# Half of an instance norm's stores moved from ScalarE's queue to GpSimd's

## The chip, the core and the metric

The kernel runs on one core of a Trainium2 chip. The metric is the device time of one execution in microseconds; the lower the better.

## The reference

`x` has the shape (4, 8, 16, 256, 256) in float32, that is 512 channels of 65,536 values, 134 MB in all. Every channel is brought to mean 0 and variance 1, and multiplied by its gamma.

```python
mu = x.mean(axis=(3, 4), keepdims=True)
var = ((x - mu) ** 2).mean(axis=(3, 4), keepdims=True)
x_norm = (x - mu) / np.sqrt(var + 1e-5)
out = x_norm * gamma[None, :, :, None, None]
```

## The kernel before

The 512 channels are cut into 32 units (`U`) of 16 channels. A unit is a tile of 128 partitions x 8192 floats (4 MB, one contiguous row of 32 KB for each partition): eight partitions hold one channel. Six tiles in SBUF, `slots` (`xt` in the profile), are used in turn: unit `u` lives in slot `u % 6`, and `AHEAD` is 6.

A unit goes through these steps:

1. Load (L48, in the helper `load`). The first six loads are issued at the start: units 0, 2, 4 and 5 by SP (SyncE), 1 and 3 by ACT (ScalarE). Every later load is issued by SP.
2. DVE (VectorE) sums each row (L107) while ACT squares it and sums the squares (L108; the squares themselves go to `junk`).
3. A small matmul with `navg` (L116) adds up the eight partitions of a channel, which gives minus the mean and minus the mean square.
4. DVE, ACT and DVE make the variance (L117), its root (L121), the reciprocal (L125) and the scale (L127), all 128 x 1.
5. DVE adds minus the mean and multiplies by the scale, in place (L130).
6. The store (L134) is issued by ACT, on ACT's queue.
7. SP issues the load of unit `u + 6` into the same slot (L136), which has to wait until the store of `u` has landed.

The order is the program's, engine by engine: nothing is moved by a scheduler, and semaphores are set where data depends on data. SP, ACT and GpSimd each have a DMA queue of their own; SP's and ACT's are listed in the profile as hardware queues (q1 and q10), GpSimd's as a software queue (q0). All three are served by the same 16 DMA engines. GpSimd's queue carries two small transfers at the start: `touch`, 16 rows of 512 B written into the output's first tile (L54) ahead of that tile's store, and `g_row`, the load of gamma (L55). After its six loads are issued, the program has 60 no-ops on ACT.

Of the kernel before, what the change touches and what calls it, by code (L numbers as in the profile page):

```python
# [1 line left out]

# [4 lines left out]

F32 = mybir.dt.float32
U8 = mybir.dt.uint8
ALU = mybir.AluOpType  # L10
ACTF = mybir.ActivationFunctionType
AX = mybir.AxisListType


@with_exitstack
def kernel(
    ctx: ExitStack,
    tc: tile.TileContext,
    x: bass.AP,
    gamma: bass.AP,  # L20
    out: bass.AP,
):
    nc = tc.nc
    B, G, C, H, W = x.shape
    P = nc.NUM_PARTITIONS
    HW = H * W
    n_ch = B * G * C
    S = 8
    K = P // S
    F = HW // S  # L30
    U = n_ch // K
    NG = (G * C) // K
    AHEAD = 6
    assert HW % S == 0 and (G * C) % K == 0

    xv = x.rearrange("b g c h w -> (b g c h w)").rearrange("(u p f) -> u p f", p=P, f=F)
    ov = out.rearrange("b g c h w -> (b g c h w)").rearrange("(u p f) -> u p f", p=P, f=F)
    gv = gamma.rearrange("g c -> (g c)")

    data = ctx.enter_context(tc.tile_pool(name="data", bufs=1))  # L40
    singles = ctx.enter_context(tc.tile_pool(name="singles", bufs=1))
    psum = ctx.enter_context(tc.tile_pool(name="psum", bufs=4, space=bass.MemoryType.PSUM))
    ctx.enter_context(tc.manual_schedule())

    slots = [data.tile([P, F], F32, name=f"xt{i}") for i in range(AHEAD)]

    def load(u, queue):
        queue.dma_start(out=slots[u % AHEAD][:], in_=xv[u])  # L48


    g_row = singles.tile([1, G * C], F32, name="g_row")
    touch = singles.tile([16, 128], F32, name="touch")
    nc.vector.memset(touch[:], 0.0)  # L53
    nc.gpsimd.dma_start(out=ov[0][0::S, 0:128], in_=touch[:])  # L54
    nc.gpsimd.dma_start(out=g_row[:], in_=gv[None, :])  # L55
    for u in range(AHEAD):
        load(u, nc.scalar if u in (1, 3) else nc.sync)

    for _ in range(60):
        nc.scalar.nop()  # L60

    eps_t = singles.tile([P, 1], F32, name="eps_t")
    nc.gpsimd.memset(eps_t[:], 1e-5)
    one = singles.tile([1, 1], F32, name="one")
    nc.gpsimd.memset(one[:], 1.0)
    navg = singles.tile([P, K, S], F32, name="navg")
    nc.gpsimd.memset(navg[:], -1.0 / HW)  # L67
    nc.gpsimd.affine_select(  # L68
        out=navg[:], in_=navg[:], pattern=[[-S, K], [0, S]], compare_op=ALU.is_ge,
        fill=0.0, base=0, channel_multiplier=1,  # L70
    )
    nc.gpsimd.affine_select(  # L72
        out=navg[:], in_=navg[:], pattern=[[S, K], [0, S]], compare_op=ALU.is_ge,
        fill=0.0, base=S - 1, channel_multiplier=-1,
    )
    navg_w = navg[:].rearrange("p k s -> p (k s)")
    root_eps = singles.tile([P, 1], F32, name="root_eps")
    nc.scalar.activation(out=root_eps[:], in_=eps_t[:], func=ACTF.Sqrt)  # L78
    g_rep = singles.tile([1, NG, K, S], F32, name="g_rep")
    g_ps = psum.tile([P, NG], F32, name="g_ps", bufs=1)  # L80
    g_col = singles.tile([P, NG], F32, name="g_col")

    nc.vector.tensor_copy(  # L83
        out=g_rep[:],
        in_=g_row[:].rearrange("o (n k) -> o n k", n=NG).unsqueeze(3).to_broadcast([1, NG, K, S]),
    )
    for n in range(NG):
        nc.tensor.matmul(  # L88
            out=g_ps[:, n : n + 1],
            lhsT=g_rep[:, n].rearrange("o k s -> o (k s)"),  # L90
            rhs=one[:],
            start=True, stop=True,
        )
    nc.vector.tensor_copy(out=g_col[:], in_=g_ps[:])  # L94

    junk = singles.tile([P, F], U8, name="junk")

    st = singles.tile([P, U, 2], F32, name="st")
    nvar = singles.tile([P, U], F32, name="nvar")
    std = singles.tile([P, U], F32, name="std")  # L100
    rstd = singles.tile([P, U], F32, name="rstd")
    scale = singles.tile([P, U], F32, name="scale")

    squares = []
    for u in range(U):
        t = slots[u % AHEAD]
        nc.vector.reduce_sum(out=st[:, u, 0:1], in_=t[:], axis=AX.X)  # L107
        square = nc.scalar.activation(  # L108
            out=junk[:], in_=t[:], func=ACTF.Square, accum_out=st[:, u, 1:2],
        )  # L110
        if u:

            tc.declare_no_dep(square.ins, squares[-1].ins, reason="junk, ordered by the root between")
        squares.append(square)
        ps = psum.tile([P, 2], F32, name="ps")
        nc.tensor.matmul(out=ps[:], lhsT=navg_w, rhs=st[:, u], start=True, stop=True)  # L116
        nc.vector.tensor_scalar(  # L117
            out=nvar[:, u : u + 1], in0=ps[:, 0:1], scalar1=ps[:, 0:1],
            scalar2=ps[:, 1:2], op0=ALU.mult, op1=ALU.add,
        )  # L120
        nc.scalar.activation(  # L121
            out=std[:, u : u + 1], in_=nvar[:, u : u + 1], func=ACTF.Sqrt,
            bias=eps_t[:], scale=-1.0,
        )
        nc.vector.reciprocal(out=rstd[:, u : u + 1], in_=std[:, u : u + 1])  # L125
        g = u % NG
        nc.vector.tensor_mul(  # L127
            out=scale[:, u : u + 1], in0=rstd[:, u : u + 1], in1=g_col[:, g : g + 1],
        )
        nc.vector.tensor_scalar(  # L130
            out=t[:], in0=t[:], scalar1=ps[:, 0:1], scalar2=scale[:, u : u + 1],
            op0=ALU.add, op1=ALU.mult,
        )
        nc.scalar.dma_start(out=ov[u], in_=t[:])  # L134
        if u + AHEAD < U:
            load(u + AHEAD, nc.sync)  # L136


# [1 line left out]
_INS = ['x', 'gamma']  # L140
_OUTS = [((4, 8, 16, 256, 256), 'float32')]


# [23 lines left out]
```

## Time and profile before

| | us |
|---|---|
| runs of the kernel: lowest, median, highest | 626.88, 627.39, 627.53 |
| profiled execution: span from the first to the last instruction | 624.9 |
| profiled execution: its own time around the span | not recorded; the runs' median is 2.5 above the span |
| busy in the span: DVE | 443.4 (71%) |
| busy in the span: ACT | 238.8 (38%) |
| busy in the span: PE (matmul) | 21.4 (3%) |
| busy in the span: POOL (GpSimd) | 2.4 (0%) |
| bytes moved by DMA | 268.46 MB, mean 430 GB/s |

How to read it: the busy times are means over the whole span. The slices show where in the span an engine or the DMA was busy, each slice being a fortieth of it (15.6 us). The DMA issues are listed by what they write and read, and by the engine that issues them (SPq, ACTq, POOLq), with the median time from issue to landing; that time holds the wait in the queue as well as the transfer.

### The profile page before, as it was taken

What the parts mean: (1) busy time and instruction counts of PE and PEld (TensorE: products, weight loads), DVE (VectorE), ACT (ScalarE), POOL (GpSimd) and SP (SyncE); (2) the same over time, 40 slices, a digit from 0 to 9 for tenths busy, and PEclk for the clock granted to TensorE, in tenths of its full rate; (3) what the DMA queues carried; (4) which work ended last, traced back from release to release, by engine and by line L of the source; (5) the groups of instructions that cost most, each with busy time, mean ns of one, the idle gap of its engine ahead of it and who ended that gap; (6) DMA issues with size and microseconds to landing.
All of it is one profiled execution on the core that took longest, in us unless ns stands there. A gap on an engine that the chain in (4) does not pass through costs nothing.

```text
span 624.9 us, 631 instructions
## 1 busy us (share of the span) xinstructions
PE 21.4 (3%) x80; PEld 19.5 (3%) x80; DVE 443.4 (71%) x163; ACT 238.8 (38%) x98; POOL 2.4 (0%) x11
## 2 busy tenths in 40 slices
PE   0200000000000000000000000000000000000000
PEld 0200000000000000000000000000000000000000
DVE  0588999999776687666786767867668676687730
ACT  0444444444443234432344423444224442244400
POOL 1000000000000000000000000000000000000000
DMA  8999999999999999999999999999999999999998
GB/s 370 436 426 430 422 434 436 436 436 437 432 424 433 436 436 424 436 436 434 436 436 432 422 436 436 434 426 436 436 434 436 436 434 419 436 436 434 426 436 369
DMA packets 9282, 268.46 MB, mean 430 GB/s; under 512 B 1072, under 2 KB 1088, under 8 KB 1088
## 3 DMA queue, kind: packets, MB, share of 16 engines
q10 hardware_dynamic: 4896, 142.61, 52.9%
q1 hardware_dynamic: 4320, 125.83, 46.8%
q0 software_dynamic: 64, 0.01, 0.0%
q14 instruction: 2, 0.02, 0.0%
HBM read 134.22 MB, written 134.23 MB: 430 GB/s over the span
## 4 chain that ended last, share of the span: by engine, by line
another core or an unknown queue 61%; DMA 17%; DVE 15%; SPq 1%; PE 1%; issue 0%; ACT 0%
DVE st L107 10%; DMA xt<-in_x_dram 10%; DMA out_dram<-xt 8%; DVE xt L130 5%; SPq L48 1%; PE ps L116 1%; ACT std L121 0%; DVE nvar L117 0%; DVE rstd L125 0%; DVE scale L127 0%
## 5 line engine op out<-in xcount | busy, mean ns | idle before, releaser
L107 DVE TENSOR_REDUCE st<-xt 128x1 f32<-128x8192 f32 x32 | 277.9, 8685 | 100.4 <-DMA xt<-in_x_dram 100.4
L108 ACT ACTIVATE junk<-xt 128x8192 uint8<-128x8192 f32 x32 | 225.0, 7030 | 275.1 <-DMA xt<-in_x_dram 231.9
L130 DVE TENSOR_SCALAR xt<-xt,ps,scale 128x8192 f32<-128x8192 f32 x32 | 145.6, 4550 | 1.2
L121 ACT ACTIVATE std<-nvar,eps_t 128x1 f32<-128x1 f32 x32 | 9.4, 294 | 79.6 <-DVE nvar L117 79.6
L116 PE MATMUL ps<-st,navg 128*128 128x2 f32 x64 | 17.9, 349 | 557.1 <-DVE st L107 557.1
L116 PEld LDWEIGHTS ps<-st,navg 128*128 128x128 f32 x64 | 16.0, 311 | 558.9 <-issue 558.9
L117 DVE TENSOR_SCALAR nvar<-ps 128x1 f32<-128x1 f32 x32 | 9.2, 287 | 23.8 <-PE ps L116 23.8
L125 DVE RECIPROCAL rstd<-std 128x1 f32<-128x1 f32 x32 | 5.2, 164 | 11.6 <-ACT std L121 11.6
L83 DVE COPY g_rep<-g_row 1x1024 f32<-1x1024 f32 x1 | 0.7, 681 | 14.3 <-DMA g_row<-in_gamma_dram 14.3
L108 ACT ACTIVATION_READ_ACCUMULATOR junk<-xt 128x1 f32 x32 | 6.0, 186 | 0.0
L127 DVE TENSOR_TENSOR scale<-rstd,g_col 128x1 f32<-128x1 f32 x32 | 5.1, 159 | 1.1
L88 PE MATMUL g_ps<-one,g_rep 1*128 1x1 f32 x16 | 3.5, 347 | 16.1 <-DVE g_rep L83 16.1
L88 PEld LDWEIGHTS g_ps<-one,g_rep 1*128 1x128 f32 x16 | 3.5, 325 | 16.1 <-issue 16.1
L94 DVE COPY g_col<-g_ps 128x8 f32<-128x8 f32 x1 | 0.2, 166 | 3.7 <-PE g_ps L88 3.7
L78 ACT ACT_TABLE_LOAD x1 | 1.3, 1283 | 1.7 <-PEq L151 1.7
L53 DVE MEMSET touch<- 16x128 f32 x1 | 0.2, 165 | 0.9 <-PEq L151 0.9
L54 POOL DMA_DIRECT2D out_dram<-touch x1 | 0.6, 619 | 0.8 <-DVE touch L53 0.8
L55 POOL DMA_DIRECT2D g_row<-in_gamma_dram x1 | 0.5, 487 | 0.0
L68 POOL TENSOR_SCALAR_AFFINE_SELECT navg<-navg 128x128 f32<-128x128 f32 x1 | 0.4, 400 | 0.1
L72 POOL TENSOR_SCALAR_AFFINE_SELECT navg<-navg 128x128 f32<-128x128 f32 x1 | 0.4, 399 | 0.1
L67 POOL MEMSET navg<- 128x128 f32 x1 | 0.2, 232 | 0.0
L78 ACT ACTIVATE root_eps<-eps_t 128x1 f32<-128x1 f32 x1 | 0.2, 203 | 0.0
(6 smaller groups left out, 0.6 us busy)
## 6 DMA issues: line engine op xcount, KB each, us to landing
out_dram<-xt ACTq DMA_DIRECT2D x32, 4096.0 KB, 62.5
xt<-in_x_dram SPq DMA_DIRECT2D x30, 4096.0 KB, 38.5
xt<-in_x_dram ACTq DMA_DIRECT2D x2, 4096.0 KB, 31.5
out_dram<-touch POOLq DMA_DIRECT2D x1, 8.0 KB, 9.1
g_row<-in_gamma_dram POOLq DMA_DIRECT2D x1, 0.5 KB, 13.3
```

The lines of the kernel that those rows point to most:

```text
L48: queue.dma_start(out=slots[u % AHEAD][:], in_=xv[u])
L78: nc.scalar.activation(out=root_eps[:], in_=eps_t[:], func=ACTF.Sqrt)
L83: nc.vector.tensor_copy(out=g_rep[:], in_=g_row[:].rearrange("o (n k) -> o n k", n=NG).unsqueeze(3).to_broadcast([1, NG, K, S]),)
L88: nc.tensor.matmul(out=g_ps[:, n : n + 1], lhsT=g_rep[:, n].rearrange("o k s -> o (k s)"), rhs=one[:], start=True, stop=True,)
L107: nc.vector.reduce_sum(out=st[:, u, 0:1], in_=t[:], axis=AX.X)
L108: square = nc.scalar.activation(out=junk[:], in_=t[:], func=ACTF.Square, accum_out=st[:, u, 1:2],)
L116: nc.tensor.matmul(out=ps[:], lhsT=navg_w, rhs=st[:, u], start=True, stop=True)
L117: nc.vector.tensor_scalar(out=nvar[:, u : u + 1], in0=ps[:, 0:1], scalar1=ps[:, 0:1], scalar2=ps[:, 1:2], op0=ALU.mult, op1=ALU.add,)
L121: nc.scalar.activation(out=std[:, u : u + 1], in_=nvar[:, u : u + 1], func=ACTF.Sqrt, bias=eps_t[:], scale=-1.0,)
L125: nc.vector.reciprocal(out=rstd[:, u : u + 1], in_=std[:, u : u + 1])
L127: nc.vector.tensor_mul(out=scale[:, u : u + 1], in0=rstd[:, u : u + 1], in1=g_col[:, g : g + 1],)
L130: nc.vector.tensor_scalar(out=t[:], in0=t[:], scalar1=ps[:, 0:1], scalar2=scale[:, u : u + 1], op0=ALU.add, op1=ALU.mult,)
```

## The change

The store of an odd unit is now issued by GpSimd, on its own queue. The store of an even unit is issued by ACT as before. The 60 no-ops on ACT are gone. Loads, tiles, arithmetic and all the rest stay, and so do the waits that data asks for: a store waits for its L130, the load of unit `u + 6` for the store of unit `u`.

```diff
     for u in range(AHEAD):
         load(u, nc.scalar if u in (1, 3) else nc.sync)
-
-    for _ in range(60):
-        nc.scalar.nop()
...
             op0=ALU.add, op1=ALU.mult,
         )
-        nc.scalar.dma_start(out=ov[u], in_=t[:])
+        (nc.gpsimd if u % 2 else nc.scalar).dma_start(out=ov[u], in_=t[:])
         if u + AHEAD < U:
             load(u + AHEAD, nc.sync)
```

GpSimd's list of instructions grows by 16 stores, behind what it did before (units 1, 3, ... 31, in this order); ACT's gets shorter by the same 16.

## The prediction

> **What bounds the kernel now.** I read the page's slices first, because DVE at 71% and ACT at 38% name no bound.
>
> ```profile
> DMA  8999999999999999999999999999999999999998
> GB/s 370 436 426 430 422 434 436 436 436 437 432 424 433 436 436 424 436 436 434 436 436 432 422 436 436 434 426 436 436 434 436 436 434 419 436 436 434 426 436 369
> ...
> q10 hardware_dynamic: 4896, 142.61, 52.9%
> q1 hardware_dynamic: 4320, 125.83, 46.8%
> q0 software_dynamic: 64, 0.01, 0.0%
> ```
>
> The 16 DMA engines are full in all but the first and last slice. q1 is SP's queue (30 loads), q10 is ACT's (32 stores, 2 loads), and q0, GpSimd's, has almost nothing. In the trace's packet records a packet is one row of 32 KB and takes 1.213 us; the first starts at 1.80 us and the last ends at 623.6. 8192 of them on 16 engines are 512 x 1.213 = 621.1 us, against a window of 621.8. So there is nothing to win in the middle: a change can only open gaps, or close 0.7 us. Next, the queues:
>
> ```profile
> out_dram<-xt ACTq DMA_DIRECT2D x32, 4096.0 KB, 62.5
> xt<-in_x_dram SPq DMA_DIRECT2D x30, 4096.0 KB, 38.5
> ```
> ```profile
> SPq L48 <- DMA out_dram<-xt: 534.4, 26, 59.5
> ```
>
> A unit comes every 19.36 us (period of SP's issues in the chain of waits), so a 4 MB transfer alone takes 19.36 / 2 = 9.68 us. A slot spends 38.5 us on its load, 15.1 in compute and 62.5 on its store: 116.1 us, which is 6 x 19.36. The second line says that SP waits only for stores, as each load needs its slot emptied. Hence 62.5 / 19.36 = 3.2 stores and two loads are outstanding at any time. Then the end, from the timeline:
>
> ```profile
> 585.26 8.69 DVE L107 TENSOR_REDUCE st<-xt 128x1 f32<-128x8192 f32 x1 [4.35 <-DMA xt<-in_x_dram]
> ...
> 595.73 4.55 DVE L130 TENSOR_SCALAR xt<-xt,ps,scale 128x8192 f32<-128x8192 f32 x1
> 600.32 0.34 ACTq L134 DMA_DIRECT2D out_dram<-xt  x1
> ```
> ```profile
> DMA to landing us min/median/max: 23.6/62.5/62.6
> ```
>
> The last load lands at 585.24. Unit 31 is computed in 15.08 us and its store issued at 600.32; it has the shortest landing, 23.6 us, so it lands at 623.9. From 585.24 to there are 38.7 us = 4.0 stores of 9.68. That is the pile of stores 28 to 31. It keeps the engines full while unit 31 is computed: the long store queue is the cover of the tail.
>
> **The change, part by part.**
>
> *No-ops.* ACT issues its second load by 1.68 us, starts its table load at 1.72, and then waits 19.4 us for the first tile (`ACT junk` row of the waits). Whatever 60 no-ops cost there, that wait hides it: 0.
>
> *Sequencers.* An issue on ACT took 0.34 us; 16 leave it. ACT also no longer waits at odd units for L130 before it squares the next tile. Its square (7.03 us) starts with DVE's reduction (8.69 us) and ends earlier, so nothing follows from that: 0. GpSimd has 2.4 us of work, all before 4 us, so its stores queue behind nothing but their own wait for L130. SP's list stays as it is: load u+6 waits for store u, in order.
>
> *Who gets turns.* This is the part that counts. The trace of before has one place with all three queues at work, the start:
>
> ```profile
> 1.35 0.62 POOL L54 DMA_DIRECT2D out_dram<-touch  x1 [0.85 <-DVE touch L53]
> ```
>
> Its 16 small rows (and those of g_row behind them) go out in the packet records one per engine every 2.43 us, between one 32 KB packet of q1 and one of q10. So the engines give each queue with work one packet in turn, and the software queue is a third partner. Before, loads and stores had one queue each and shared 1:1 however long the store pile was, so the pile built at the start (units 0 to 5 were finished 14.93 us apart) stayed to the end. With stores in two queues, two outstanding stores get two turns of three: they drain at two per 3 x 9.68 = 29.0 us, while a new store comes only with each load, one per 29.0 us. The pile loses one store each 29 us until one is in flight; 2.2 surplus stores are gone in some 64 us, long before the end. From then on the share is 1:1, a unit still takes 19.36 us, and the six slots hold the difference as waiting loads: stores land after about 20.7 us (even) to 24.3 (odd), loads after 116.2 - 15.1 - 22.5 = 78.6. The middle costs nothing, but the cover of the tail is gone.
>
> *How late a software store starts.* A hardware load issued at 0.80 had its first packet at 1.80: 1.0 us. The software store issued at 1.35 had its first packet at 7.12; its turn at 4.70 passed unused, so it was ready 3.4 to 5.8 us after issue. That was 16 rows; with 128, the 0.62 us of its instruction may grow eightfold, by 4.3 us, or not at all. The ends are 1.0 (as hardware) and 5.8 + 4.3 = 10.1 us; I take 4.6, the middle of the only row of its kind.
>
> The Trainium skill ("DMA: Bandwidth & Descriptors", section "Latency and other measured facts") gives a first byte after about 1 us for GpSimd's path and 0.6 for the others. By that difference of 0.4 us the sum below would be about +8.7 us instead of +11.2; the touch row, at 3.4 or more, disagrees.
>
> *The tail.* At the last load's landing, these stores are still to be moved:
> - store 31: 9.68 us, not issued;
> - store 30 (even, ACT): issued 19.36 - 15.08 = 4.28 us before, started 1.0 later, half of 3.28 us moved: 8.1 left;
> - store 29 (odd, GpSimd): issued 23.6 us before, started 4.6 later; half of 15.7 and a third of 3.28 moved, 9.0 in all: 0.7 left.
>
> That is 18.5 us of work instead of 38.7. The engines were full up to there in both cases, so the last load lands 38.7 - 18.5 = 20.2 us later, at 605.4. After it come 15.08 us of compute, 4.6 to start, 9.68 of data and 0.35 to land: 29.7 us instead of 38.7. Net: +20.2 - 9.0 = **+11.2 us**. Seen as a gap: the engines run dry 8.8 us after the last load and get store 31 after 19.7, so they idle 10.9 us. With a start of 1.0 us the same lines give +21.0 - 12.6 = +8.4; with 10.1, +17.5 - 3.5 = +14.0.
>
> *Sum.* On the profiled span: 624.9 + 11.2 = 636.1. The median of the runs, 627.39, is 2.5 us above the span; that part stays, so 638.6 us.
>
> **Rivals.**
>
> *Nothing changes (the side that is not slower).* The store pile could outlive the split, if the software queue gets fewer turns than a third of them (by the row above it got exactly its turn, but with packets too small to matter). The place is the tail. The point is 15.08 + 4.6 = 19.7 us, or 2.0 stores, still queued besides store 31 when the last load lands; my sum leaves 8.8 us, before had 29.0. From there on the bytes set the end: 627.4. In its favour: the 62.5 us of landing show how deep that pile is today.
>
> The Trainium skill (same page, "Issuing engines are not separate DMA queues") says that issuing from several engines only saves the sequencer's issue time; read by itself it forecasts this case. The trace agrees on the shared engines, and shows beside it that the number of queues sets the share.
>
> *Software packets smaller than a row.* If 32 KB rows are cut into k packets, the odd stores get 1/k of a turn, their pile stays, and the tail is mostly covered; but each packet costs about 8 ns more (the 512-byte packets took 27 ns, their bytes at 27 GB/s take 19). 128 odd rows per engine x (k-1) x 8 ns: 3.1 us at k=4, 7.2 at k=8; at k=2 1 us and a good half of the gap, some 6. So 630.5 to 635. Against it: touch went out as whole rows of 512 B; for it: no row of before shows a large software packet.
>
> *Software stores start far later.* If making 128 rows' descriptors takes eight times the touch store's time and more, each odd store holds its slot longer, and store 31 pays it in full: +14.0 and above, 641.4 to 646. For it: 5.8 us were possible with 16 rows. Against: the instruction itself took only 0.62 us.
>
> *Faster.* By over 0.2% (1.25 us, about what a measurement can tell here) would need more than the 0.7 us of slack in the DMA window, so packets under 1.21 us.
>
> **How the numbers follow.** Forecast 0.68, at 638.6 (635.8 to 641.4 by the start's ends); small packets 0.12; late start 0.12; no change 0.06; faster 0.02. The range leaves out the no-change and faster cases (0.08), about half of the small packets and the far end of the late starts: 632 to 645. Slower by over 0.2%: 0.68 + 0.12 + 0.12 = 0.92; within it 0.06; faster 0.02.
>
> **What would show it.** Right: the middle slices still at 430 to 436 GB/s; loads landing after some 77 us and stores after 20 to 27, even ones sooner than odd; the last reduction starting near 605; about 11 us without DMA traffic before the last store. The chain of waits should end in L107, L130 and the last store. A last reduction near 585 would refute the turns; a span of unit periods above 19.36 in the middle would mean slower packets; q0 packets far above 2,368 (16 x 128 rows and 16 x 16 completions, beside the 64 of before) would mean cut rows. The prediction is wrong as a whole if the last slices stay full.

## The result, and the profile after

The changed kernel takes 668.7 us (median of four runs, 666.9 to 673.7) against 627.26 for the kernel before on the same chip (median of four, three of which stand in the table of before): a ratio of 1.0675, 95% interval 1.0635 to 1.0715. The forecast was 638.6 us, with 645 as the upper end. The direction and the place (loads pile up, stores get short, the tail opens) came out as forecast; the size did not: +41 us instead of +11.

The profiled execution took 673.7 us, the slowest of the four, with a span of 671.7. First the slices of its page:

```profile
DMA  9999999999999999999999999999999999975465
GB/s 375 437 406 412 423 412 420 398 410 435 436 425 412 418 427 433 418 412 416 423 435 420 412 421 410 435 425 429 421 427 416 425 418 410 433 332 256 207 258 250
```

Two things differ from before. The tail is open, but over five slices of 16.8 us instead of one gap of 11 us. And the middle, with engines as full as before, moves 398 to 437 GB/s instead of 419 to 437. Next the transfers, with their median time from issue to landing:

```profile
xt<-in_x_dram SPq DMA_DIRECT2D x30, 4096.0 KB, 81.9
out_dram<-xt ACTq DMA_DIRECT2D x16, 4096.0 KB, 26.2
out_dram<-xt POOLq DMA_DIRECT2D x16, 4096.0 KB, 27.5
```

The store pile is gone and waits as loads, near the forecast (78.6 for loads, 20.7 and 24.3 for stores). Then the end, in the timeline:

```profile
603.42 8.69 DVE L104 TENSOR_REDUCE st<-xt 128x1 f32<-128x8192 f32 x1 [3.13 <-DMA xt<-in_x_dram]
...
624.05 8.69 DVE L104 TENSOR_REDUCE st<-xt 128x1 f32<-128x8192 f32 x1 [5.61 <-DMA xt<-in_x_dram]
...
643.42 8.69 DVE L104 TENSOR_REDUCE st<-xt 128x1 f32<-128x8192 f32 x1 [4.34 <-DMA xt<-in_x_dram]
...
658.74 0.53 POOL L131 DMA_DIRECT2D out_dram<-xt  x1 [39.47 <-DVE xt L127]
```

The last reduction starts at 643.4, not near 605. Of the 11 us forecast without DMA traffic before the last store, 7.1 are found (652.7 to 659.8 in the packet records). The last three tiles come some 20 us apart, while by stretches (the last two columns are the DMA share and GB/s) the engines idle:

```profile
240.00:400.00 160.00, 4.47 (x16) 4.01 (x16) 107.17 (x41) 57.23 (x23) 2.12 (x4) 1.00 1.00 422
...
585.00:600.00 15.00, 0.56 (x2) 0.50 (x2) 13.55 (x5) 7.42 (x3) 0.00 (x0) 1.00 0.75 326
600.00:640.00 40.00, 1.12 (x4) 1.01 (x4) 27.99 (x11) 14.83 (x6) 0.53 (x1) 1.00 0.57 245
640.00:672.00 32.00, 0.56 (x2) 0.50 (x2) 13.85 (x5) 7.42 (x3) 0.53 (x1) 1.00 0.60 257
```

At 422 GB/s the share is still 1.00: packets take longer, the engines are not starved. The packet records show how. A 32 KB packet took 1.216 us on average before and 1.246 after; before, 42 packets took more than 1.26 us (called *long* here, the first 6 us left out), after, 709, up to 2.67 us, over twice 1.213. And the engines go apart. A load counts its 16 engines in, one by one. Before, the first and last of the 16 were at most about 1 us apart; after, the distance grows along the run, to 58.4 us at the last load: the first engine had its rows of unit 31 at 585.0, where all had them before, the last at 643.4.

So the 46.8 us between the spans split, per engine, into longer packets, 512 x (1.246 - 1.216) = 15.6, and idle time. The latter was 15 x 0.25 + 40 x 0.43 + 32 x 0.40 = 33.8 us after, against 2.5 in the last 25 us before: 31.3. The forecast had 0 and 10.9.

### The profile page after: what moved, and what is told of

It reads as the page before. It is cut to its first block, busy times and chain, and to the rows that moved or that the text cites. A ratio compares the mean times of both kernels' runs of the same rounds, so it can differ in the third digit from the quotient of the medians.

```text
span 671.7 us, 618 instructions
## 1 busy us (share of the span) xinstructions
PE 21.4 (3%) x80; PEld 19.5 (3%) x80; DVE 443.7 (66%) x163; ACT 238.6 (36%) x98; POOL 10.9 (2%) x27
## 3 DMA queue, kind: packets, MB, share of 16 engines
q10 hardware_dynamic: 2592, 75.50, 26.5%
q0 software_dynamic: 2368, 67.12, 24.3%
## 4 chain that ended last, share of the span: by engine, by line
issue 68%; DVE 21%; another core or an unknown queue 4%; DMA 3%; POOL 1%; PE 1%; ACT 0%; POOLq 0%
DVE st L104 13%; DVE xt L127 7%; DMA xt<-in_x_dram 3%; POOL out_dram L131 1%; PE ps L113 1%; ACT std L118 0%; DVE nvar L114 0%; DVE rstd L122 0%; DVE scale L124 0%; POOLq L159 0%; POOLq L131 0%
## 5 line engine op out<-in xcount | busy, mean ns | idle before, releaser
L131 POOL DMA_DIRECT2D out_dram<-xt x16 | 8.6, 534 | 647.0 <-DVE xt L127 647.0
## 6 DMA issues: line engine op xcount, KB each, us to landing
xt<-in_x_dram SPq DMA_DIRECT2D x30, 4096.0 KB, 81.9
out_dram<-xt ACTq DMA_DIRECT2D x16, 4096.0 KB, 26.2
out_dram<-xt POOLq DMA_DIRECT2D x16, 4096.0 KB, 27.5
```

Source lines behind the costliest of these rows:

```text
L131: (nc.gpsimd if u % 2 else nc.scalar).dma_start(out=ov[u], in_=t[:])
```

## Experiments

Times are medians, in us; ratios are to the runs of the kernel before on the same chip, with the 95% interval; they are worked out over all runs and are not exactly the quotients of the medians. Long packets are counted from 6 us on; the spread is the largest distance between the first and the last engine of one load in the second half of the run. Landings are medians from issue.

| run | time | ratio | stores land | loads land (SP) | long | spread |
|---|---|---|---|---|---|---|
| before | 627.3 | | 62.5 | 38.5 | 42 | 1 |
| after | 668.7 | 1.0675 (1.0635 to 1.0715) | 26.2, 27.5 | 81.9 | 709 | 59 |
| no-ops dropped | 626.9 | 0.9997 (0.9986 to 1.0008) | 62.5 | 38.5 | 35 | 1 |
| all stores on GpSimd | 628.5 | 1.0023 (1.0012 to 1.0034) | 62.2 | 38.5 | 50 | 1.4 |
| three tiles, ACT stores | 660.8 | 1.0540 (1.0509 to 1.0570) | 21.4 | 22.9 | 460 | 5 |
| split up to unit 15 | 659.7 | 1.0522 (1.0491 to 1.0552) | 29.6, 29.3 | 71.4 | 564 | 51 |
| extra rows at the start | 640.9 | 1.0219 (1.0190 to 1.0249) | 65.4 | 27.7 | 78 | 5 |
| split, four tiles | 661.0 | 1.0540 (1.0492 to 1.0589) | 24.7, 26.5 | 39.3 | 451 | 24 |
| split, other unit order | 668.6 | 1.0662 (1.0596 to 1.0728) | 27.6, 28.0 | 79.3 | 614 | 54 |
| odd loads on GpSimd | 627.3 | 1.0005 (0.9994 to 1.0017) | 69.6 | 25.7, GpSimd 27.8 | 60 | 2 |
| store 1 on GpSimd | 632.5 | 1.0097 (1.0046 to 1.0148) | 47.9 | 53.3 | 277 | 8 |
| stores 1, 3 on GpSimd | 643.6 | 1.0268 (1.0238 to 1.0298) | 28.7 | 72.9 | 368 | 19 |
| four tiles, ACT stores | 632.0 | 1.0082 (1.0052 to 1.0111) | 35.1 | 27.2 | 94 | 1 |
| split from unit 24 | 649.1 | 1.0359 (1.0338 to 1.0379) | 62.5, 32.7 | 38.5 | 445 | 10 |

The diffs below are against the kernel named with them.

### No-ops dropped, alone (to before)

```diff
-    for _ in range(60):
-        nc.scalar.nop()
```

> The 60 no-ops dropped, nothing else. All theories: no change, 627.4 us within 0.2%. If the no-ops matter, a part of the 41 us shows here.

Measured: 0.9997. The no-ops are worth nothing, as forecast; the 41 us are the stores'.

### All stores on GpSimd (to after)

```diff
-        (nc.gpsimd if u % 2 else nc.scalar).dma_start(out=ov[u], in_=t[:])
+        nc.gpsimd.dma_start(out=ov[u], in_=t[:])
```

> All 32 stores on GpSimd's queue, so stores have one queue again. Turns theory (two store queues drain the pile, the tail loses its cover): one store queue keeps its pile, so stores land after 60 us or more, loads after some 36, and the time is 627.4 plus at most 4 us. Software theory (transfers from the software queue lengthen packets, on some engines more than on others, and the engines drift apart): twice the software packets, so at least as slow as the changed kernel, 668 us and more. Restart theory (a store queue that runs empty and starts anew with every unit makes the engines get into each other's way, on whichever queue): the pile keeps the queue from running empty, so 627 to 632 us.

Measured: 628.5 us, 50 long packets. The issues of this kernel:

```profile
out_dram<-xt POOLq DMA_DIRECT2D x32, 4096.0 KB, 62.2
xt<-in_x_dram SPq DMA_DIRECT2D x30, 4096.0 KB, 38.5
```

Twice the software stores, and the time of before within 0.3%: the software theory falls. Moving all stores to the software queue costs 1.5 us, not 41. With one queue the stores keep their pile, and packets stay short; whether they stay short because of the pile this run does not show.

### Three tiles, all stores on ACT (to before)

```diff
-    AHEAD = 6
+    AHEAD = 3
```

> The kernel before with three tiles in SBUF instead of six: all stores on ACT's hardware queue, but the pile is short (3 x 19.36 - 15.1 leaves 43 us for a load and a store, 21 each), so the store queue runs empty with every unit. Turns theory, by the same turn-by-turn sum: the tail's gap of 8 us and 9 us of gaps at the start, some 644 us. Software theory: no software stores, so packets stay at 1.21 us and the engines together, 644 us. Restart theory: longer packets and engines apart as in the changed kernel, clearly above 644 us (655 or more), with load landings spread over the engines by more than 5 us.

Measured: 660.8 us, 17 above the turns theory, with 460 long packets, no software queue in play past the first 25 us. That is the time that the restart theory gave (655 or more), though the spread of 4.8 us stays below its 5. So long packets are not bound to GpSimd. Here 454 of the 460 are loads, in stretches such as 287 to 294 us, where all 16 engines had only loads, some in the rows of one unit and some in the next.

### Split up to unit 15, ACT's queue from there on (to after)

```diff
-        (nc.gpsimd if u % 2 else nc.scalar).dma_start(out=ov[u], in_=t[:])
+        (nc.gpsimd if u % 2 and u < 16 else nc.scalar).dma_start(out=ov[u], in_=t[:])
```

> The changed kernel, but from unit 16 on all stores go to ACT's queue again. The short store pile persists by the turn-by-turn sum, as one queue against one shares 1:1. Turns theory: 635 us. Software theory: packets above 1.26 us end when the software stores end, near 330 us, and about half of the excess of 41 us stays: some 645 to 650 us. Restart theory: long packets and drift go on after unit 16 as before it, some 665 us.

Measured: 659.7 us, between the software and the restart theories. The last software store was issued at 331 us, and its last packet started at 354; 69, 45 and 39 long packets follow in the three stretches of 40 us from 360 on, with one load queue and one store queue, both hardware. Why they are long is not shown. Then come 3 in all from 480 to 600. The spread settles at 47 us and stays there to the end, without growing and without closing, and is paid in the tail (a DMA share of 0.60 after 600 us). So from 480 us on engines that are apart do no harm by themselves, but nothing brings them together again.

### Extra rows at the start (to before)

```diff
+    for i in (2, 4, 5):
+        nc.sync.dma_start(out=slots[i][0:8], in_=xv[i][0:8])
     for u in range(AHEAD):
         load(u, nc.scalar if u in (1, 3) else nc.sync)
```

> The kernel before, its queues and its long store pile untouched, with three extra loads of 8 rows of 32 KB at the very start, one row for each of 8 engines (3.6 us more work for those 8, nothing for the others), so half of the engines run three rows behind the other half. Restart theory (a queue that runs empty and starts anew makes packets long): no queue runs empty, packets stay at 1.21 us, 627 to 631 us. Step theory (the engines are only undisturbed while all go through the same rows at the same time; once they are out of step they hinder each other, and some fall behind): packets above 1.26 us all along instead of some 40, engines further and further apart, 640 us or more.

Measured: 640.9 us, but not for the reason expected. The packet records show 48 packets, the 24 extra rows among them, that take 3.2 to 4.6 us each, 4.0 on average (the extra rows are 8 rows close together in SBUF, fetched by 8 engines at once; why that is slow is not shown). By 22 us the engines have finished 87 rows of the tiles instead of 252, which is some 12 of the 14 us. From there on half of the engines run 3 to 5 us behind the others for 600 us, with 4 long packets. The plain step theory falls: being 3 to 5 us out of step, with one load queue and one store queue, lengthens nothing.

### Split, with four tiles (to after)

```diff
-    AHEAD = 6
+    AHEAD = 4
```

> The changed kernel with four tiles in SBUF instead of six: loads can only pile up 42 us deep instead of 81, so an engine can lead another by one load less or two. Turns theory: 637 us. Theory that the slowest engine's lag, summed up behind a deep load pile, is what is paid at the end: the landings of one load spread over the engines by at most some 20 us, and the time is between 637 and 660. If the depth of the load pile does not matter: 665 us and more.

Measured: 661.0 us, just above the second case (637 to 660). The spread is held at 23 to 24 us by the shorter load pile, yet the time falls by only 8 us. A deep load pile lets engines lead each other; it is not what costs most of the time.

### Split, other unit order (to after)

```diff
+    PERM = [i // 2 + 16 * (i % 2) for i in range(32)]
...
-        queue.dma_start(out=slots[u % AHEAD][:], in_=xv[u])
+        queue.dma_start(out=slots[u % AHEAD][:], in_=xv[PERM[u]])
```

(the stores and gamma's column go by `PERM` too)

> The changed kernel, going through the units in the order 0, 16, 1, 17, 2, 18 and so on, so that the store and the load that share the engines are 16 units (64 MB) apart in memory instead of one. If the addresses of the load and the store that run side by side make the long packets: their number falls from some 700 to under 100 and the time to about 636 us. Step and restart theories: no change, 655 to 675 us.

Measured: 668.6 us, 614 long packets. The distance in memory between the units that share the engines is not the cause.

### Odd loads on GpSimd, all stores on ACT (to before)

```diff
-            load(u + AHEAD, nc.sync)
+            load(u + AHEAD, nc.gpsimd if u % 2 else nc.sync)
```

> The mirror image: all stores on ACT's queue, odd loads from unit 7 on on GpSimd's, so loads have two queues and two turns of three. Turns theory: the load pile is drained, the store pile grows to 79 us of landing and covers the tail: 627 us. Restart and step theories: now the load queues run empty with every unit, packets above 1.26 us come by the hundred; but the short load pile holds the engines together: 635 to 660 us.

Measured: 627.3 us. The issues show the mirror image of the change:

```profile
out_dram<-xt ACTq DMA_DIRECT2D x32, 4096.0 KB, 69.6
xt<-in_x_dram SPq DMA_DIRECT2D x17, 4096.0 KB, 25.7
xt<-in_x_dram POOLq DMA_DIRECT2D x13, 4096.0 KB, 27.8
```

Three queues, loads with two of them, the load pile drained, the store pile longer than before, and no loss. The turns theory has the time right (627); the store pile grew less than it summed (69.6 us of landing, not 79). Neither a third queue nor a queue that runs empty costs anything where it is the loads'.

### Store 1, or stores 1 and 3, on GpSimd (to after)

```diff
-        (nc.gpsimd if u % 2 else nc.scalar).dma_start(out=ov[u], in_=t[:])
+        (nc.gpsimd if u == 1 else nc.scalar).dma_start(out=ov[u], in_=t[:])
```

> The changed kernel with store 1 alone on GpSimd's queue, the other 31 on ACT's. By the turn-by-turn sum this takes one store out of the pile: stores land after 45 us (2.3 stores outstanding), enough to cover the tail: 627 us. Theory of the short pile (packets get long only while the store queue can run empty on some engines): the same, 627 to 629 us, hardly a long packet after 100 us. If any use of a third queue starts a disturbance that then feeds itself: 640 us and more.

The second run has `u in (1, 3)` there.

> Stores 1 and 3 on GpSimd's queue, the other 30 on ACT's. Turn-by-turn sum: stores land after 28.5 us (1.5 outstanding), the tail opens by 4.4 us: 631 us. Theory of the short pile: 1.5 stores are at the edge of running empty, some long packets, 631 to 655 us. If the number of software stores matters: 2 of 16, so 627 + 41/8 = 632 us.

Measured: 632.5 us (630.9 to 637.5 in five runs), between the cases of its expectation, and 643.6, inside the range of the short pile. The pile drains as summed: stores land after 47.9 (45 summed) and 28.7 us (28.5). But one 32nd of the stores on another queue costs 5.6 us. With store 1 alone on GpSimd, 155 of the 277 long packets fall between 40 and 120 us; the software store's own packets run from 59 to 83 us. A rest of some 10 in each 40 us goes on with one load queue and one store queue, nearly all of them loads, and more towards the end (2 from 120 to 160 us, 26 from 560 to 600). This rest is not explained.

### Four tiles, all stores on ACT (to before)

```diff
-    AHEAD = 6
+    AHEAD = 4
```

> The kernel before with four tiles in SBUF instead of six, all stores on ACT's queue: two stores outstanding (40 us), one load (21 us). Turn-by-turn sum: 1.8 us of a gap at the start, 629 us. Theory of the short store pile: two stores outstanding do not run empty, 629 to 631 us, hardly a long packet after 100 us; with the split at four tiles the time was 661 us. If it is the number of tiles that makes packets long: near 661 us.

Measured: 632.0 us, 3 above the turn-by-turn sum, 80 of the 94 long packets between 40 and 120 us. With four tiles the split costs 29 us (661.0 against 632.0): four tiles instead of six are not the cause either.

### Split from unit 24 on (to after)

```diff
-        (nc.gpsimd if u % 2 else nc.scalar).dma_start(out=ov[u], in_=t[:])
+        (nc.gpsimd if u % 2 and u >= 24 else nc.scalar).dma_start(out=ov[u], in_=t[:])
```

> The changed kernel with the split from unit 24 on: units 0 to 23 store on ACT's queue, then 25, 27, 29 and 31 on GpSimd's. By the turn-by-turn sum the store pile is gone within five units (landing 75 us at unit 24, 20 at unit 28), the last load lands 20.6 us later than before, and the tail opens by 8.3 us (with a software store starting 1.3 us after its issue, as the changed kernel's last store did): 635 us. If turns and tail are as summed and the rest of the 41 us is collected unit by unit while the pile is short: 635 to 640 us, long packets only after 500 us. If turns do not drain the pile: 627 to 629. If the split costs its whole price as soon as the pile is gone: 650 us and more.

Measured: 649.1 us, above the 635 to 640 of the mixed case. The first software store is issued at 484.67, and the stretches turn there (last column GB/s):

```profile
440.00:480.00 40.00, 1.13 (x5) 1.01 (x4) 28.48 (x14) 15.13 (x7) 0.00 (x0) 1.00 1.00 433
490.00:600.00 110.00, 2.23 (x8) 2.00 (x8) 54.80 (x21) 29.07 (x13) 1.07 (x2) 1.00 1.00 391
620.00:648.00 28.00, 0.56 (x2) 0.50 (x2) 12.98 (x5) 6.55 (x3) 0.53 (x1) 1.00 0.55 233
```

From 433 to 391 GB/s at a full share, 0% to 29% long packets, and of the software packets 88%. It begins at once, while ACT's pile is still three stores deep and the engines are within 1.0 us of one another (the spread of the loads up to there). So neither an empty queue at ACT nor engines far apart are needed for a start. GpSimd's queue does start anew with every store here; the restart theory falls only with the next run, where all queues are kept filled.

This run also shows the mix come and go. The packets of the first software store run from 490 to 522 us and those of the second from 545 to 577. In these stretches 45% (490 to 524) and 41% (544 to 580) of the packets are long; between them, from 530 to 544 us, with loads and ACT's stores alone, none of 184 is. The pile drained more slowly than summed: unit 28's store landed after 40.7 us, not 20.

The 110 us at 391 instead of 433 cost 110 x (1 - 391/433) = 10.7 us; with the 8.3 of the turns that is 19 of the 22 us.

### Six mixes of queues, transfers alone

No computation, one execution; loads and stores of whole tiles, each stage's queues kept filled:

```python
phase([sp], [act], 6)          # loads on, stores on, transfers of each
phase([sp], [pool], 4)
phase([sp], [act, pool], 6)
phase([sp, act], [pool], 4)
phase([], [act, pool], 3)
phase([sp, act], [], 4)
```

> Only transfers, no computation (it leaves the whole of it out): six stages, each with its queues kept filled and parted by waits. Stage 1: loads on SP, stores on ACT. 2: loads on SP, stores on GpSimd. 3: loads on SP, stores on ACT and on GpSimd. 4: loads on SP and ACT, stores on GpSimd. 5: stores on ACT and GpSimd, no loads. 6: loads on SP and ACT, no stores. Measured: the share of 32 KB packets above 1.26 us in each stage. If a third queue in the engines' turns makes packets long, by itself: stages 3 and 4 have 5 to 15% long packets, the others under 2%. If it takes two store queues beside loads: stage 3 alone. If it takes a queue that runs empty: under 2% everywhere but in the first and last rows of a stage. If two queues of the same direction side by side do it: 3 to 6.

```profile
30.00:130.00 100.00, 0.06 (x1) 0.00 (x0) 1.00 1.01 434
150.00:210.00 60.00, 0.18 (x3) 0.00 (x0) 1.00 1.00 431
240.00:400.00 160.00, 0.06 (x1) 0.00 (x0) 1.00 1.00 358
450.00:520.00 70.00, 0.06 (x1) 0.00 (x0) 1.00 1.00 430
560.00:640.00 80.00, 0.00 (x0) 0.00 (x0) 1.00 1.01 430
```

These are stretches inside stages 1 to 4 and, the last line, of stages 5 and 6, which ran into each other so that there too loads ran beside two store queues. Long packets: 0.4%, 0.3%, 46%, 3.4%, 2.4%. Loads beside two store queues move 358 GB/s, 17% less, at a full share: software stores take 1.83 us, loads 1.34, ACT's stores 1.21 as ever. The three queues get the same number of turns (585, 582 and 583 packets on SP's, ACT's and GpSimd's). It is the mix itself, without tiles that wait, drain or compute, and without a queue that runs empty. Yet the last line has the same mix without the loss: of the software packets 5% are long there, 86% in the stretch of stage 3. (The next expectation gives 2% and 70% for them.) The packet records differ in one point: there all 16 engines are mostly on one queue together and turn to the next together, while at 300 us they are spread over the three, 4, 2 and 10 on SP's, ACT's and GpSimd's.

### Seven mixes, engines put out of step

```python
phase([sp], [act], 4)
phase([sp], [pool], 4)
phase([], [act, pool], 4)
phase([], [sp, act], 4)
phase([sp, act], [], 4)
phase([sp, act], [pool], 4)
phase([sp], [act, pool], 2)
```

One execution. Each stage begins with a load of 8 rows of 14 KB.

> Only transfers, no computation (it leaves the whole of it out). In the run with six stages, the two spans of time with loads and two store queues came out opposite: 70% of the software packets long where the engines were mixed over the three queues, 2% where all 16 turned to the same queue together. Here each stage opens with 8 small extra rows that hold up 8 of the 16 engines by some 2 us, so that the engines are out of step from the start. Stages: 1 loads on SP, stores on ACT; 2 loads on SP, stores on GpSimd; 3 stores on ACT and GpSimd; 4 stores on SP and ACT; 5 loads on SP and ACT; 6 loads on SP and ACT, stores on GpSimd; 7 loads on SP, stores on ACT and GpSimd. Share of packets above 1.26 us: if being out of step is enough, all stages over 5%. If it takes a software and a hardware queue moving the same way (rows dealt to the engines differently): stages 3 and 7 over 5%, 4 and 5 under 2%. If it takes any two stores side by side out of step: 3, 4 and 7. If it takes three queues: 6 and 7 alone.

```profile
190.00:250.00 60.00, 0.00 (x0) 0.00 (x0) 1.00 1.00 432
...
440.00:540.00 100.00, 0.06 (x1) 0.00 (x0) 1.00 1.00 433
560.00:610.00 50.00, 0.06 (x1) 0.00 (x0) 1.00 1.00 413
```

The lines are stages 3 (two store queues, no loads), 6 (two load queues, one store queue) and 7 (one load queue, two store queues). Long packets once a stage runs: 0%, 7%, 0%, 0%, 0%, 0% and 25%. None of the four cases of the expectation fits whole; the one for any two stores side by side comes nearest, but wants the loads as well. Of the mixes run, two store queues beside a load queue is the one that suffers most; stores alone, loads alone, and two load queues beside one store queue do not. For the last of these the engines were as spread as in stage 3 of the run before: at 450 us, in stage 6, 7, 3 and 6 of the 16 were on SP's, ACT's and GpSimd's queues. Stage 4 says less: at 280, 300 and 320 us 15 or 16 engines were on the same queue. Stage 2 (7%, loads beside software stores) is a weak case of its own.

## Why the prediction failed in size

- **No-ops, sequencers, order on SP.** Right: 0.
- **Turns by queue.** Right. Loads land after 81.9 us, stores after 26.2 and 27.5 (78.6, 20.7 and 24.3 forecast), even ones sooner than odd. With transfers alone three queues got 585, 582 and 583 packets. In the other runs the landings follow the turn-by-turn sum within 3 us in three cases (45 summed and 47.9 measured, 28.5 and 28.7, 21 and 21.4 with three tiles) and miss it by more in three others (79 and 69.6, 40 and 35.1, 20 and 40.7).
- **"The middle costs nothing."** This is the step that failed. It took every packet as 1.213 us whatever the mix of queues, since the trace of before shows only one load queue beside one store queue. With the stores on two queues packets get longer: 1.246 us on average instead of 1.216, which is 15.6 us per engine in the profiled run, and up to 2.67. The prediction had named the sign, unit periods above 19.36 us: from unit 8 to unit 27 the reductions start 21.0 us apart. Two store queues working beside the loads are enough to lengthen packets (358 GB/s with transfers alone, and the stretches of the split from unit 24 on). They are not the whole of it here: between 100 and 585 us of the changed kernel 10% of the packets are long while a software store is moved, and 9% while none is.
- **"The engines were full up to there in both cases."** The same failure, second half. The long packets do not fall evenly. The slowest engine ended its loads 58 us after the first, and each tile waits for its slowest engine. The last load came 58.2 us later than before (643.42 - 585.26) where the sum had 20.2.
- **The tail after the last load.** Forecast 29.7 us instead of 38.7, measured 26.7 (643.4 to the landing at 670.1). The start of the last software store was over-sized: it landed 11.4 us after its issue, of which 9.68 and 0.35 are data and landing, so it started after some 1.3 us, not 4.6 (its first packet is recorded 1.1 us after the issue; that of ACT's last store 0.84). The Trainium skill's figure ("DMA: Bandwidth & Descriptors", section "Latency and other measured facts"), 0.4 us later than hardware, was the better one for the tail. The row from the start of the kernel seems to have measured full engines rather than the software queue: as long as the engines were full, up to some 565 us, the changed kernel's stores on an empty queue had their first packet 3.6 to 6.0 us after issue on GpSimd's queue, and 3.4 to 4.3 on ACT's, for which the prediction had 1.0. This is part of why the even stores land 5.5 us later than forecast.
- **Together.** +58.2 - 12.0 = +46.2 us to the last landing, against +20.2 - 9.0. One slip in the sum is small: store 30 was given half of the 3.28 us in which three queues work, store 29 a third. A third for both makes the forecast +10.7 instead of +11.2.
- **The rivals.** Packets stayed whole rows (q0 has 2,368 packets, the count of uncut rows). A late start of the software stores is not what the tail paid for (1.1 us). The rule of the Trainium skill (the same page, section "Issuing engines are not separate DMA queues"), that issuing from several engines only saves the time of issuing, is what the trace disagrees with: 358 GB/s against 434 and 431 when the second store queue is added. It holds for the two mixes without a loss (all stores on GpSimd, odd loads on GpSimd: 1.0023 and 1.0005).

**What stays open.** Why packets get long, on the memory's or on SBUF's side, is not shown. Shown not to be needed or not to be enough: software stores as such, the order of the units in memory, engines 3 to 5 us out of step with two queues, a store queue running empty, a third queue. In every run with two store queues beside loads one of the two was GpSimd's; two hardware store queues beside loads were not run, so it is not shown whether it takes the software queue as one of the two. That it takes engines spread over the queues (some on one, some on another at the same time) *and* two store queues beside loads rests on two stretches of one run and one stage of another. Not explained by it are the long loads with three tiles, on hardware queues alone, the 153 long packets from 360 to 480 us in the split up to unit 15, the rest with store 1 on GpSimd, and the long packets of the changed kernel while no software store is moved.

## What to carry to other kernels

Where the DMA engines are full, the number of queues is a choice of shares: every queue with work gets one packet in turn, so a second queue for stores drains the stores and piles up the loads, and the pile that covered the compute of the last tile is gone. In this kernel one queue for each direction was best, and a third did no harm when it was given to the loads (1.0005). A DMA share of 1.00 does not say that the engines run at their rate (it was seen from 358 to 434 GB/s here): read GB/s beside it, and the spread of a transfer's 16 engines.

## What the runs showed of the hardware that was not expected

- Loads beside two store queues: 358 GB/s instead of 430 to 434, packets up to 2.71 us instead of 1.213, at a full share.
- Engines that had come apart did not come together again: 47 us of distance held from 480 to 600 us, almost without long packets (split up to unit 15).
- How soon a store starts was set by how busy the engines were more than by the kind of queue: with full engines and an empty queue the first packet came 3.6 to 6.0 us after issue on GpSimd's queue and 3.4 to 4.3 on ACT's, at the end 1.1 and 0.84 (the changed kernel).
- Eight rows close together in SBUF, loaded by eight engines at once: 3.2 to 4.6 us for a row instead of 1.21 (extra rows at the start).
